# Second block, second layer: mixing by blocks of 128 tokens inside the expert stages, and modulation sums on VectorE

## The chip, the core and the metric

The kernel runs on one core of one Trainium2 chip. The time is that of the device for one execution, in microseconds (us). The engines are TensorE (PE, its weight loads PEld), VectorE (DVE), ScalarE (ACT), GpSimd (POOL) and SyncE (SP, which issues the plain DMAs). All arithmetic that matters is fp32.

## What is computed

A first block (two layers of a transformer over 256 tokens and 256 context tokens, 1024 features) is followed by a second block of two layers. What matters here:

```python
# first block, each layer: shifts, scales and gates from the conditioning vectors
m = silu(cond) @ w_mod + b_mod            # 6 parts of 1024, for c and for c_ctx
h = rms_norm(x, norm_mix) * (1 + sc1) + sh1

# second block, each of 2 layers, x is 256 x 1024
x = x + mixing(rms_norm(x, norm1_g))      # 3 kinds of heads, all causal, then w_out
x = x + peer(rms_norm(x, norm2_g))

# mixing: z = xn @ w_in; 6 stick-breaking attention heads, 6 mLSTM heads in
# chunks of 128 (with a causal conv of width 4 ahead), 4 spatial gating groups in chunks of 128

# peer (the expert layer), for each token and each of 8 heads
q = xn @ wq;  scores against two sets of 128 keys
top 16 of each, top 16 of their 256 sums -> 16 experts idx and gate = softmax
act = xn . u[idx];  w = gelu(act) * gate;  y += sum_k w[k] * v[idx[k]]
```

Every part of the mixing is causal or works within 128 tokens: tokens 0 to 127 never need anything of tokens 128 to 255. The expert layer treats each token by itself.

## The kernel before

**Program.** The first block (to about 1000 us) is written stage by stage. The second block is `block2` (L759): for each layer `mixing` (L765), `norm2_first` (L742) and `peer` (L1076), one after another. The order of the mixing of a layer is a written list (`MIXING`, L1246); it works on all 256 tokens with features on partitions, and each weight tile is split into two halves of fp32r that are multiplied in three passes (`mm3`, L169 to L171; the split on ACT L133 and DVE L134).

**Expert layer** (`peer`). It goes over 2 token blocks times 8 heads times 8 pairs. A pair is two gathers on POOL (L1152), each bringing for 128 tokens one expert's row of u and v (8 KB a token, 1.05 MB a gather) into one of the 8 `b16` buffers, of which two are held for the layer, so that 6 serve the gathers. DVE multiplies u by the tokens, held in the PSUM tile `xt`, and sums (L1156). `weigh` (L1131), one pair behind, makes the gelu'd and gated weight a diagonal matrix on ACT (L129, tile `lo`), and PE adds weight times v onto the two banks `y` (L1140, four matmuls of 512 columns). The lists of experts of a head come from `routed` (L1116) and `route` (L1202, some 30 small DVE instructions); for the first block of tokens `scores` (L1098) also multiplies two weight tiles, loaded through the three `raw` buffers. Two heads are routed before the first pair, each other two heads ahead. `peer_out` (L1171) turns y into the feature layout and adds it to x. Nothing of the next layer's mixing starts before that.

**Modulation** of the first block. Parts 0 and 1 of layer 0 (`mod_first`, L222) are computed inside the first layer's start, with the weights `w_mod0` loaded there. Parts 2 to 5 of layer 0 (`mod_step`, L246) are 32 weight tiles that are fed one by one between other stages, each by two PE matmuls with two stationary columns (L264). Layer 1's parts go through `mod_sum` (L270): DVE multiplies each tile by a column and adds (L126), and only the sums over partitions are matmuls (L288). `mod_out` (L292) transposes the result and adds the bias. `pow_rsqrt` (L314) is the inverse root, a power on POOL (L319).

**Order.** Each engine runs its instructions in the order of its own list; the lists are made when the program is built, by a scheduler that may move an instruction ahead of others in program order.

Of the kernel before, what the change touches and what calls it, by code (L numbers as in the profile page):

```python
# [19 lines left out]
P = 128  # L20
# [46 lines left out]
class Kernel:  # L67
    def __init__(self, tc, ctx, d, out):
        self.tc, self.nc, self.d, self.out = tc, tc.nc, d, out
        self.n = 0  # L70
        self.ahead = []
        self.hold = []
        self.pool = ctx.enter_context(tc.tile_pool(name="sb", bufs=1))
        self.pp = ctx.enter_context(tc.tile_pool(name="ps", bufs=1, space=bass.MemoryType.PSUM))
        self.pp2 = self.scope = None
        self.psum_pool()
# [6 lines left out]
    def psum(self, tag):  # L83
        pool = self.pp2 if tag == "sm" else self.pp
        return pool.tile([P, 512], F32, tag=tag, name=self.name(tag), bufs={"mm": 3, "sm": 4, "ax": 1}[tag])
# [55 lines left out]
    def raw(self, ap):  # L141
        n = ap.shape[-1]
# [71 lines left out]
    def mod_setup(self):  # L214
# [5 lines left out]
        self.mod_ps = None  # L220

    def mod_first(self, q):  # L222

        w = self.b16([P, KD, 512])
        for k in range(0, KD, 4):
            self.nc.sync.dma_start(w[:, k:k + 4], self.d["w_mod0"][q, :, k:k + 4])
        ps = self.psum("ax")
# [6 lines left out]
        pt = self.psum("mm")  # L234
        for j in range(4):
            self.transpose(pt[:, j * P:(j + 1) * P], rows[:, j * P:(j + 1) * P])
        p4 = pt.rearrange("p (c j r) -> p c j r", c=2, r=P)
        blk = slice(2 * q, 2 * q + 2)
        mod = self.mods[0][:, :2, blk]
        self.tt(mod, p4[:, :, :, :2], self.b_mod[:, 0, :2, blk, None].to_broadcast([P, 2, 2, 2]), OP.add)  # L240
        for g in range(32, P, 32):
            self.tt(mod, p4[:, :, :, g:g + 2], mod, OP.add)
        g = self.cols["norm_mix"]
        self.stt(mod[:, 1], mod[:, 1], 1.0, g[:, 0, blk, None].to_broadcast([P, 2, 2]), OP.add, OP.mult)

    def mod_step(self, n=1):  # L246


        for _ in range(n):
# [5 lines left out]
            if l:  # L255
                self.mod_sum(l, c, k)
                continue
            if k == 0:
                self.mod_ps = self.psum("ax")
                self.nc.vector.memset(self.mod_ps, 0.0)  # L260
            w = self.raw(self.d["w_mod"][self.mod_pos - 17])
# [4 lines left out]
            if k < 7:  # L266
                continue
            self.mod_out(l, c, lambda p3, half: [p3[:, :, 32 * half + o:32 * half + o + 2] for o in (0, 64)])

    def mod_sum(self, l, c, k):  # L270

        if k == 0:
            self.mod_acc = self.s8([P, 2, D])
        w = self.raw(self.d["w_mod"][self.mod_pos - 17])
        acc = self.mod_acc
        for i in range(2):
            if k == 0:
                self.ts(acc[:, i], w, self.sc[:, k, i:i + 1], None, OP.mult)
            else:
                self.stt(acc[:, i], w, self.sc[:, k, i:i + 1], acc[:, i], OP.mult, OP.add)  # L280
# [4 lines left out]
        for i in range(2):  # L285
            for half in range(2):
                g = 32 * (2 * half + i)
                self.nc.tensor.matmul(self.mod_ps[g:g + 1, :], self.ones[:, :1],  # L288
                                      acc[:, i, half * 512:half * 512 + 512], start=True, stop=True)
        self.mod_out(l, c, lambda p3, half: [p3[:, :, 64 * half:64 * half + 64:32]])  # L290

    def mod_out(self, l, c, parts):  # L292
# [7 lines left out]
        mod = self.mods[l][:, c]  # L300
        for half in range(2):
            m = mod[:, 4 * half:4 * half + 4]
            add = self.b_mod[:, l, c, 4 * half:4 * half + 4, None].to_broadcast([P, 4, 2])
            for part in parts(p3, half):
                self.tt(m, part, add, OP.add)
                add = m
        if c in (1, 4):
# [1120 lines left out]
```

## Time and profile before

| quantity | value |
|---|---|
| median of 3 runs | 2931.26 us (2930.69 to 2934.92) |
| the profiled execution | 2938.2 us |
| its span, first to last instruction | 2936.4 us |
| PE, DVE, ACT, POOL busy | 87%, 66%, 36%, 19% of the span |
| mean granted clock of PE | 0.968 |
| moved by DMA | 776.35 MB, of it 536.90 MB by the gathers |

The first block ends at about 1000 us, the mixing of layer 0 takes until about 1340 us, the gathers of layer 0 run from 1380.2 us to 2053 us, the mixing of layer 1 lies between, and the gathers of layer 1 run from 2243 us to the end. The busy shares are means over stages with different limits, so a stage is read from the slices and windows below, and the reason for a wait from the groups of instructions, where each line ends with the idle time ahead of it and what released it.

### The profile page before, as it was taken

Reading aid. Unit: us, or ns where it says so; the run is one execution under the profiler, and the core shown is the slowest. Engines: PE = TensorE matmul, PEld = TensorE weight load, DVE = VectorE, ACT = ScalarE, POOL = GpSimd, SP = SyncE. Lnnn points to the kernel's source line nnn. Section 1 sums busy time; section 2 is a strip of 40 time slices with the busy share of each in tenths; the row PEclk is TensorE's granted clock in tenths of the full one; section 3 lists DMA queues with packets and bytes.
Section 4 is the critical chain, followed back from the end, with each engine's and each line's share of the span. In section 5 each row is a group of like instructions: output and inputs, shape, how many; then the busy total and the mean of one; then the engine's idle time right before and its main releaser. Section 6 shows DMA issues by size and latency. Waiting matters only on the chain.

```text
span 2936.4 us, 33987 instructions
## 1 busy us (share of the span) xinstructions
PE 2565.1 (87%) x11870; PEld 1750.2 (60%) x11870; DVE 1937.0 (66%) x4272; ACT 1057.4 (36%) x2173; POOL 551.1 (19%) x559
## 2 busy tenths in 40 slices
PE   6999999999999999997788878777997888687777
PEld 4666777888788999986444323322886444232222
DVE  4434659997375887577667769555577776975554
ACT  3333334442264565464323323111554332421111
POOL 0000000000000000102343333332112333233332
PEclk9999999999999999999999998999998999989999
DMA  6432235555343456433999999999426999889998
GB/s 247 144 134 86 79 110 191 187 189 175 115 138 108 155 185 200 150 108 139 418 418 419 418 420 395 419 420 384 132 72 242 418 418 419 349 360 420 420 420 354
DMA packets 140569, 776.35 MB, mean 264 GB/s; under 512 B 15728, under 2 KB 18800, under 8 KB 73328
## 3 DMA queue, kind: packets, MB, share of 16 engines
q0 software_dynamic: 73728, 536.90, 44.4%
q1 hardware_dynamic: 66672, 237.28, 24.2%
q8 instruction: 95, 1.56, 0.2%
q14 instruction: 74, 0.61, 0.1%
HBM read 773.08 MB, written 1.05 MB: 264 GB/s over the span
## 4 chain that ended last, share of the span: by engine, by line
PE 29%; DMA 23%; DVE 14%; ACT 2%; issue 2%; POOL 1%; POOLq 0%; ACTq 0%; DVEq 0%; SPq 0%
DMA b<-in_peer_uv_dram,b 20%; PE y L1140 8%; PE mm L169 5%; PE mm L170 5%; PE mm L171 5%; DVE b L1156 5%; DMA raw<-in_peer_wq_dram 4%; DVE t L117 2%; PE sm L45 1%; DVE t L1197 1%; DVE b L1200 1%; PE mm L45 1%; DVE b L1199 1%; ACT hi L133 1%; DVE lo L134 1%
## 5 line engine op out<-in xcount | busy, mean ns | idle before, releaser
L1140 PE MATMUL y<-b,lo 128*128 128x512 f32 x2048 | 976.7, 628 | 279.8 <-ACT lo L129 279.8
L1140 PEld LDWEIGHTS y<-b,lo 128*128 128x128 f32 x2048 | 394.8, 200 | 832.6 <-issue 418.9
L1156 DVE SCALAR_TENSOR_TENSOR b<-xt,b 128x1024 f32<-128x1024 f32 x512 | 620.0, 1221 | 273.8 <-DMA b<-in_peer_uv_dram,b 271.6
L1152 POOL DMA_INDIRECT b<-in_peer_uv_dram,b x512 | 500.5, 978 | 854.2 <-DMA b<-in_peer_uv_dram,b 347.5
L134 DVE TENSOR_TENSOR lo<-raw,hi 128x1024 fp32r<-128x1024 f32 (+1 forms) x339 | 406.1, 1199 | 298.9 <-ACT hi L133 269.9
L133 ACT ACTIVATE hi<-raw 128x1024 fp32r<-128x1024 f32 (+1 forms) x339 | 351.8, 1039 | 562.3 <-PE mm L170 278.4
L169 PE MATMUL mm<-b,hi 128*128 128x512 f32 (+1 forms) x1512 | 528.6, 351 | 4.0 <-ACT b L129 1.5
L170 PE MATMUL mm<-b,hi 128*128 128x512 f32 (+1 forms) x1512 | 525.3, 348 | 0.0
L171 PE MATMUL mm<-b,lo 128*128 128x512 f32 (+1 forms) x1512 | 525.1, 348 | 0.0
L319 POOL TENSOR_TENSOR c<-c,k_mhalf 128x4 f32<-128x4 f32 (+2 forms) x39 | 45.1, 1156 | 1502.4 <-DVE c L123 1501.6
L169 PEld LDWEIGHTS mm<-b,hi 128*128 128x128 f32 x1512 | 285.8, 189 | 54.8 <-issue 6.5
L171 PEld LDWEIGHTS mm<-b,lo 128*128 128x128 f32 x1512 | 286.3, 189 | 37.7 <-issue 2.7
L170 PEld LDWEIGHTS mm<-b,hi 128*128 128x128 f32 x1512 | 286.3, 189 | 37.7 <-DVE b L126 2.6
L129 ACT ACTIVATE b<-b 128x2 f32<-128x2 f32 (+2 forms) x280 | 61.8, 221 | 672.5 <-DVE b L1156 664.8
L169 PE MATMUL mm<-s,hi 128*128 128x256 f32 (+2 forms) x976 | 285.4, 295 | 7.3 <-ACT s L133 5.1
L171 PE MATMUL mm<-s,lo 128*128 128x256 f32 (+2 forms) x976 | 282.5, 293 | 0.0
L170 PE MATMUL mm<-s,hi 128*128 128x256 f32 (+2 forms) x976 | 280.4, 289 | 0.9 <-DVE s L134 0.6
L129 ACT ACTIVATE lo<-k_sq,b 128x128 f32<-128x128 f32 x512 | 178.6, 394 | 179.2 <-DVE b L117 173.8
L169 PEld LDWEIGHTS mm<-s,hi 128*128 128x128 f32 (+1 forms) x976 | 188.2, 194 | 17.0 <-ACT s L133 6.8
L170 PEld LDWEIGHTS mm<-s,hi 128*128 128x128 f32 (+1 forms) x976 | 188.3, 193 | 5.6 <-issue 2.4
L171 PEld LDWEIGHTS mm<-s,lo 128*128 128x128 f32 (+1 forms) x976 | 187.8, 194 | 3.6 <-issue 2.6
L117 DVE TENSOR_TENSOR b<-b 128x2 f32<-128x2 f32 (+3 forms) x272 | 45.9, 170 | 102.5 <-ACT b L129 102.4
(241 smaller groups left out, 2361.1 us busy)
## 6 DMA issues: line engine op xcount, KB each, us to landing
raw<-in_w_in_dram SPq DMA_DIRECT2D x97, 512.0 KB, 3.4
raw<-in_w_up_dram SPq DMA_DIRECT2D x88, 512.0 KB, 3.3
raw<-in_w_mod_dram SPq DMA_DIRECT2D x80, 512.0 KB, 3.6
raw<-in_w_out_dram SPq DMA_DIRECT2D x32, 512.0 KB, 3.3
raw<-in_w_down_dram SPq DMA_DIRECT2D x32, 512.0 KB, 3.6
raw<-in_peer_wq_dram SPq DMA_DIRECT2D x32, 512.0 KB, 8.5
b<-in_w_mod_dram SPq DMA_DIRECT2D x8, 1024.0 KB, 12.4
raw<-in_w_br_dram SPq DMA_DIRECT2D x16, 512.0 KB, 3.3
```

The lines of the kernel that those rows point to most:

```text
L45: ins = k.nc.tensor.matmul(out, lhsT, rhs, start=first is None, stop=True, skip_group_check=True)
L117: self.nc.vector.tensor_tensor(out, a, b, op=op)
L129: self.nc.scalar.activation(out, in_, fn, **kw)
L133: return (self.nc.scalar.activation(hi, x, AF.Copy), self.nc.vector.tensor_tensor(lo, x, hi.bitcast(F32), op=OP.subtract))
L134: self.nc.vector.tensor_tensor(lo, x, hi.bitcast(F32), op=OP.subtract))
L169: mm(ps, sh, mh, start=first, stop=False)
L170: mm(ps, sh, ml, start=False, stop=False)
L171: mm(ps, sl, mh, start=False, stop=last)
L319: self.nc.gpsimd.tensor_tensor(r[:, :n], v[:, :n], self.mhalf[:, :n], op=OP.pow)
L1140: nc.tensor.matmul(bank["y"][c], dg[:, i], rows[:, i, D + 512 * c:D + 512 * (c + 1)], start=h == 0 and k + i == 0, stop=h == 7 and k + i = ...
L1152: nc.gpsimd.indirect_dma_start(out=rows[:, i], out_offset=None, in_=table[:, :], in_offset=bass.IndirectOffsetOnAxis(ap=part["idx"][:, tb, ...
L1156: self.nc.vector.scalar_tensor_tensor(rows[:, i, :D], bank["x"], 1.0, rows[:, i, :D], op0=OP.mult, op1=OP.mult, accum_out=part["act"][:, t ...
```

## The change

The expert layers and layer 1's mixing become four `stage`s, (layer, token block): (0,0), (0,1), (1,0), (1,1). A stage is the 64 pairs of one block; behind each pair it takes `rate` steps of a generator of other work. `first_routes` (layer 0's scores and routes) runs beside (0,0), the mixing of tokens 0 to 127 for layer 1 and their routes (`mixed(0)`) beside (0,1), those of tokens 128 to 255 (`mixed(1)`) beside (1,0). `mixed` keeps tokens on partitions, and multiplies with the weight as the moving operand in plain fp32 (`rows_product`), without the split into halves; the weights, the keys and the constants are loaded anew for each block of tokens where `mixed` asks for them. x is held token by token (`xtm`), and the expert result is added and sent from there. The `b16` tile `stream` is held too. The tokens that DVE multiplies come from SBUF (`part["x"]`) instead of PSUM.

In the first block parts 2 to 4 of layer 0's modulation become DVE sums by halves (`mod_half`) and part 5 goes by `mod_sum`; the tiles of `w_mod0` and the first three of `w_vu` are loaded at the program's start.

```diff
     def mod_step(self, n=1):
...
-            if l:
+            if l == 0 and c < 5:
+                self.mod_half(c, *divmod(k, 4))
+            else:
                 self.mod_sum(l, c, k)
-                continue
...
-            for half in range(2):
-                g = 32 * (2 * (k % 2) + half)
-                self.nc.tensor.matmul(self.mod_ps[g:g + 2, :], self.sc[:, k, :], w[:, half * 512:half * 512 + 512],
-                                      start=k < 2, stop=k >= 6)
...
+    def mod_half(self, c, half, pair):
+
+        w = self.raw(self.d["w_mod"][self.mod_pos - 17])
+        for i in range(2):
+            self.mod_add(self.mod_parts, w[:, 512 * i:512 * i + 512], 2 * pair + i)
+        if pair < 3:
+            return
...
     def block2(self, x, xn):
-        for l in range(DEPTH):
-            self.mixing(l, x, self.norm2(x, self.cols["norm1"][:, l], 3) if l else xn)
-            x = self.peer(l, x)
-            self.psum_pool(l + 1 == DEPTH)
...
+        self.mixing(0, x, xn)
+        self.experts(x)
+        self.psum_pool(True)
...
+        first = self.first_routes(x, xf, xn, q, later)
+        self.run(first, (0, 0, 1))
+        self.stage(0, 0, first, 0.5)
+        mix = [self.mixed(b) for b in range(2)]
+        self.stage(0, 1, chain(first, mix[0]), 1.5)
+        self.stage(1, 0, chain(mix[0], mix[1]), 1.6)
+        self.stage(1, 1, mix[1], 1)
...
+    def stage(self, l, tb, work, rate):
...
+        for h in range(8):
+            self.run(work, (l, tb, h))
             for k in range(0, 16, 2):
                 rows = self.b16([P, 2, 2 * D])
...
                 for i in range(2):
-                    self.nc.vector.scalar_tensor_tensor(
-                        rows[:, i, :D], bank["x"], 1.0, rows[:, i, :D], op0=OP.mult, op1=OP.mult,
-                        accum_out=part["act"][:, tb, h, k + i:k + i + 1])
+                    nc.vector.scalar_tensor_tensor(
+                        rows[:, i, :D], part["x"], 1.0, rows[:, i, :D], op0=OP.mult, op1=OP.mult,
+                        accum_out=part["act"][:, h, k + i:k + i + 1])
...
+                behind.append((h, k, rows))
+                due += rate
+                while n + 1 <= due:
+                    next(work, None)
+                    n += 1
...
+    def rows_product(self, xT, units, n, per=2):
...
+        for ap in units:
+            w = self.raw(ap)
+            for i in range(per):
+                self.nc.tensor.matmul(ps, xT[:, k], w[:, i * n:(i + 1) * n], start=k == 0, stop=k == KD - 1)
+                k += 1
+            if k < KD:
+                yield
```

How the lists of the engines change, at three places. On PE, beside the gathers of the second block of tokens of layer 0, before:

```order
L1140 MATMUL y_14315<-b_2571_14419,lo_14438 128x512
L1140 MATMUL y_14316<-b_2571_14419,lo_14438 128x512
L1140 MATMUL y_14315<-b_2571_14419,lo_14438 128x512
L1140 MATMUL y_14316<-b_2571_14419,lo_14438 128x512
L1140 MATMUL y_14315<-b_2573_14433,lo_14452 128x512
L1140 MATMUL y_14316<-b_2573_14433,lo_14452 128x512
```

The same place now (`mm` is the bank of a product, `raw` a weight tile, `s` the turned tokens):

```order
L1156 MATMUL y_14678<-b_2648_14754,lo_14778 128x512
L1156 MATMUL y_14679<-b_2648_14754,lo_14778 128x512
L1156 MATMUL y_14678<-b_2648_14754,lo_14778 128x512
L1156 MATMUL y_14679<-b_2648_14754,lo_14778 128x512
L1247 MATMUL mm_14768<-raw_14791,s_2634_14690 128x512 x2
L1247 MATMUL mm_14768<-raw_14809,s_2634_14690 128x512
L1156 MATMUL y_14678<-b_2652_14773,lo_14800 128x512
L1156 MATMUL y_14679<-b_2652_14773,lo_14800 128x512
L1156 MATMUL y_14678<-b_2652_14773,lo_14800 128x512
L1156 MATMUL y_14679<-b_2652_14773,lo_14800 128x512
```

Between the four matmuls of one pair and those of the next now stand about three of the mixing, each of which needs a weight tile that SP has loaded. On POOL, a little into the second block of tokens, before (a gather's target is a buffer `b`, two gathers each row):

```order
L1152 DMA b_2542_14262<-in_peer_uv_dram,b_2230_12417 128x2048 x2
L1152 DMA b_2552_14317<-in_peer_uv_dram,b_2230_12417 128x2048 x2
L1152 DMA b_2553_14323<-in_peer_uv_dram,b_2230_12417 128x2048 x2
L1152 DMA b_2555_14337<-in_peer_uv_dram,b_2230_12417 128x2048 x2
L1152 DMA b_2567_14391<-in_peer_uv_dram,b_2230_12417 128x2048 x2
```

And now, with the first inverse root of `mixed(0)` (`c` is a column of sums):

```order
L1164 DMA b_2620_14631<-in_peer_uv_dram,b_2240_12506 128x2048 x2
L1164 DMA b_2623_14655<-in_peer_uv_dram,b_2240_12506 128x2048 x2
L1164 DMA b_2630_14674<-in_peer_uv_dram,b_2240_12506 128x2048 x2
L333 TENSOR_TENSOR c_2628_14670<-c_2627_14668,k_mhalf_75 128x1
L1164 DMA b_2641_14712<-in_peer_uv_dram,b_2240_12506 128x2048 x2
L1164 DMA b_2644_14730<-in_peer_uv_dram,b_2240_12506 128x2048 x2
```

Its input `c_2627` is written on DVE directly behind the second multiply of b_2623, so two gathers (b_2630) are issued beyond the data that DVE has by then. There are ten such roots in the stages. On DVE, at the 51st pair of stage (0,0), before:

```order
L117 TENSOR_TENSOR b_2230_12417<-b_2230_12417 128x2
L1156 SCALAR_TENSOR_TENSOR b_2496_14000,b_2230_12417<-xt_12613,b_2496_14000 128x1024 x2
L117 TENSOR_TENSOR b_2230_12417<-b_2230_12417 128x2
L1156 SCALAR_TENSOR_TENSOR b_2508_14054,b_2230_12417<-xt_12613,b_2508_14054 128x1024 x2
L117 TENSOR_TENSOR b_2230_12417<-b_2230_12417 128x2
```

And now:

```order
L1168 SCALAR_TENSOR_TENSOR b_2554_14289,b_2240_12506<-b_2240_12506,b_2554_14289 128x1024
L119 TENSOR_TENSOR b_2240_12506<-b_2240_12506 128x2
L1647 TENSOR_REDUCE sv_14422<-t_2579_14414 128x32
L1604 MAX sv_14454<-b_2218_12390 128x8
L128 SCALAR_TENSOR_TENSOR b_2240_12506<-sv_14422 128x16
L1604 MAX sv_14454<-b_2218_12390 128x8
L1605 MATCH_REPLACE t_2586_14453<-sv_14454,b_2218_12390 128x128
L1607 MAX_INDEX b_2240_12506<-sv_14454,b_2218_12390 128x8
L1606 MAX sv_14454<-t_2586_14453 128x8
L1605 MATCH_REPLACE t_2586_14453<-sv_14454,b_2218_12390 128x128
L1608 MAX_INDEX b_2240_12506<-sv_14454,t_2586_14453 128x8
L1168 SCALAR_TENSOR_TENSOR b_2554_14289,b_2240_12506<-b_2240_12506,b_2554_14289 128x1024
```

All 16 routes of layer 0 now lie in stage (0,0), half a route beside each of 20 pairs in a row (pairs 34 to 53); before, four pairs of layer 0 near there and ten at the second block's start had so much.

## Rows read from the trace of the kernel before

**Rows 1.** Page, the span in 40 slices of 73 us: tenths, GB/s
```profile
PE   6999999999999999997788878777997888687777
DVE  4434659997375887577667769555577776975554
PEclk9999999999999999999999998999998999989999
DMA  6432235555343456433999999999426999889998
GB/s 247 144 134 86 79 110 191 187 189 175 115 138 108 155 185 200 150 108 139 418 418 419 418 420 395 419 420 384 132 72 242 418 418 419 349 360 420 420 420 354
```
**Rows 2.** Windows: busy us (x count) of PE, PEld, DVE, ACT, POOL; PEclk, DMA share, GB/s
```profile
200.00:400.00 200.00, 198.57 (x999) 150.29 (x998) 104.00 (x184) 68.34 (x120) 0.00 (x0) 1.00 0.27 91
1400.00:1500.00 100.00, 82.55 (x299) 46.75 (x298) 62.90 (x174) 30.66 (x78) 36.32 (x35) 0.95 1.02 418
1900.00:2000.00 100.00, 74.38 (x161) 28.75 (x160) 51.80 (x100) 17.93 (x60) 37.09 (x40) 1.00 1.01 420
2100.00:2200.00 100.00, 99.01 (x661) 84.81 (x660) 70.65 (x150) 57.37 (x121) 14.50 (x12) 1.00 0.30 101
2500.00:2600.00 100.00, 67.71 (x129) 27.79 (x130) 98.31 (x388) 40.71 (x86) 28.17 (x31) 0.86 0.84 327
```
**Rows 3.** Groups, 1900 to 2000 us: busy, mean ns, idle ahead and releaser
```profile
L1140 PE MATMUL y<-b,lo 128*128 128x512 f32 x161 | 74.6, 605 | 25.6 <-ACT lo L129 25.6
L1152 POOL DMA_INDIRECT b<-in_peer_uv_dram,b x40 | 37.6, 939 | 63.2 <-DMA b<-in_peer_uv_dram,b 60.0 <-issue 3.1
```
**Rows 4.** Chain between the layers: start, length, step
```profile
2052.96 1.25 DVE b L1156 x2
2250.58 1.25 DVE b L1156 x2
```
**Rows 5.** Windows of L264 alone, sum over 60 to 500 us
```profile
sum 440.00, PE 35.74 PEld 3.15; mean PE 11.91 PEld 1.05
```
**Rows 6.** Groups, 400 to 600 us
```profile
L126 DVE SCALAR_TENSOR_TENSOR s<-raw,k_sc,s 128x1024 f32<-128x1024 f32 x46 | 58.4, 1278 | 0.0
L288 PE MATMUL ax<-s,k_sq 128*1 128x512 f32 x24 | 3.1, 590 | 0.0
```
**Rows 7.** Groups of PE, 1990 to 2240 us
```profile
L138 PE MATMUL sm<-k_sq,t 128*128 128x128 f32 x28 | 5.1, 280 | 0.7 <-DVE t L114 0.7
```
**Rows 8.** Waits of PE, 0 to 80 us: in all, times, longest
```profile
PE sm L169 <- ACT b L129: 5.2, 2, 4.3
PE ax L231 <- DMA b<-in_w_mod_dram: 2.0, 3, 1.4
```
**Rows 9.** DMA, 1400 to 1600 us: queue and share; issues and us to landing
```profile
q1 hardware_dynamic: 2160, 5.90, 7.5%
raw<-in_peer_wq_dram SPq DMA_DIRECT2D x8, 512.0 KB, 8.8
```
**Rows 10.** Groups, 2500 to 2600 us
```profile
L1156 DVE SCALAR_TENSOR_TENSOR b<-xt,b 128x1024 f32<-128x1024 f32 x33 | 39.9, 1213 | 0.0
L1152 POOL DMA_INDIRECT b<-in_peer_uv_dram,b x31 | 29.1, 940 | 72.1 <-PE y L1140 60.5 <-issue 4.9 <-DVE b L1156 4.8
```
**Rows 11.** Two lines over the span: ns min/median/max, first and last start
```profile
L1152 POOL DMA_INDIRECT b<-in_peer_uv_dram,b x512: 935/939/1805, 1380.2 to 2907.0; - x171
L1156 DVE SCALAR_TENSOR_TENSOR b<-xt,b x512: 1203/1224/1227, 1386.2 to 2926.7; 128x1024 f32<-128x1024 f32 x171
```
**Rows 12.** Page, costliest groups: the power on POOL
```profile
L319 POOL TENSOR_TENSOR c<-c,k_mhalf 128x4 f32<-128x4 f32 (+2 forms) x39 | 45.1, 1156 | 1502.4 <-DVE c L123 1501.6
```
**Rows 13.** Two lines, 1500 to 1600 us: ns min/median/max
```profile
L134 DVE TENSOR_TENSOR lo<-raw,hi x4: 1210/1225/1227, 1525.3 to 1571.1; 128x1024 fp32r<-128x1024 f32 x4
L1152 POOL DMA_INDIRECT b<-in_peer_uv_dram,b x36: 935/939/1804, 1501.4 to 1595.9; - x36
```
**Rows 14.** Chain, 1390 to 1460 us: start, length, step
```profile
1398.32 11.34 DMA raw<-in_peer_wq_dram
1426.84 17.45 PE y L1140 x40
```

More of the change, by code (lines that the diff above doesn't have):

```diff
@@ L404, in block1 @@
         self.mod_setup()
+        self.mod_w, raws = [], []
+        for u in range(4):
+            self.mod_w.append(self.mod_load(u))
+            if u < 3:
+                raws.append(self.raw(d["w_vu"][0, u]))
+        self.raws = raws
         self.sink = self.sb([P, DEPTH, 8], "k_sink")
@@ L1093, in peer @@
             c += 8 * n
         for name in ("pos", "si", "idx"):
-            part[name] = part[name].bitcast(U32)
-        now = {}
-        def scores(h):
-            nonlocal q
-            c0 = 0 if h else 1
-            if h:
-                q = self.t2([P, 2, T])
-            for c in range(c0, 2):
-                self.copy(q[:, c], self.fm(self.unit(d["peer_wq"][l, 2 * h + c]), xn, 0, KD, 0, T))
-            keys = self.raw(d["peer_keys"][l, h].rearrange("p c n -> p (c n)")).rearrange("p (c n) -> p c n", c=2)
-            ps = self.psum("mm")
-            for tb in range(2):
-                for c in range(2):
-                    nc.tensor.matmul(ps[:, tb * T + c * P:tb * T + (c + 1) * P], q[:, c, tb * P:(tb + 1) * P],
-                                     keys[:, c], start=True, stop=True)
-            s = now[h] = self.t2([P, 512])
-            self.copy(s[:, :T], ps[:, :T])
-            self.copy(later[:, h], ps[:, T:])
@@ L1116, in routed @@
-        def routed(tb, h):
-            if tb == 0:
-                scores(h)
-                s = now.pop(h)
-                src, tmp = s[:, :T], s[:, T:]
-            else:
-                src, tmp = later[:, h], self.t2([P, 512])[:, :T]
-            self.route(tb, h, src, tmp, part)
-        units = [(tb, h) for tb in range(2) for h in range(8)]
-        routed(*units[0])
-        routed(*units[1])
+            self.part[name] = self.part[name].bitcast(U32)
+        self.done = set()
+        stream = self.b16([P, 4096])
@@ new lines, in experts, with run @@
+        self.xtm = stream[:, :2 * D].rearrange("p (b c) -> p b c", b=2)
+        self.kept = stream[:, 2 * D:]
+        first = self.first_routes(x, xf, xn, q, later)
[5 more added lines that the diff above has]
+        self.stage(1, 1, mix[1], 1)
+    def run(self, work, key):
+        while key not in self.done:
+            next(work)
@@ L1128, in peer, with weigh @@
+    def stage(self, l, tb, work, rate):
+        nc = self.nc
+        table = self.d[f"peer_uv{l}"]
+        part = {n: p[:, tb] for n, p in self.part.items()}
+        y = None
         behind = []
-        bank = {}
-        def weigh(tb, h, k, rows):
-            w = part["w"][:, tb, h, k:k + 2]
-            self.tt(w, w, part["e"][:, tb, h, k:k + 2], OP.mult)
+        due = n = 0.0
+        def weigh(h, k, rows):
+            w = part["w"][:, h, k:k + 2]
+            self.tt(w, w, part["e"][:, h, k:k + 2], OP.mult)
@@ L1159, in peer @@
                     if i == 0 and behind:
+                        if y is None:
+                            y = [self.pp2.tile([P, 512], F32, tag=f"y{c}", name=self.name("y"), bufs=1)
+                                 for c in range(2)]
                         weigh(*behind.pop())
-                self.act(part["w"][:, tb, h, k:k + 2], part["act"][:, tb, h, k:k + 2], AF.Gelu_apprx_tanh)
-                behind.append((tb, h, k, rows))
-                if k == 4 and n + 2 < len(units):
-                    routed(*units[n + 2])
```

537 lines of the change are left out of this document (454 added, 83 removed).

## The prediction

> **What bounds the kernel now.** I read the slices of the page first, then windows of 100 us in each stage, then groups and the chain for the waits. The slices [rows 1] show three regimes: PE full and DMA a quarter to a half used (slices 2 to 18, the first block and the first mixing); DMA full at 418 to 420 GB/s with PE at 7 or 8 tenths (the gathers of both layers); and between them, in slices 29 to 31, PE full again and DMA down to 72 GB/s. The windows say it more sharply [rows 2]: at 1900 us DMA is at 1.01, PE at 74%, DVE at 52%; at 2100 us, in the second layer's mixing, PE is at 99% and DMA at 0.30. So the program alternates between a stage that only PE holds and one that only DMA holds, and the change puts one beside the other. Inside the quiet gathers 40 land in 100 us (POOL waits 60 of 100 us for data), so a pair takes 5.0 us; PE works 74.6 us of the 100 on y, 3.73 us a pair, and waits 25.6 us for the diagonals of ScalarE, 1.28 us a pair [rows 3].
>
> **The change part by part.** The sum is made against the profiled execution, 2938.2 us; the median is 6.9 us less, and this is taken off at the end.
>
> *The gap.* The last multiply of layer 0 starts at 2052.96 and the first of layer 1 at 2250.58, 197.6 us later [rows 4]. In quiet gathers two such are 2.5 us apart (100/40), so what goes is **-195 us**. It goes whole only if the new work ends inside its stages. By the steps it does: each `mixed` yields some 90 times, and a stage of 64 pairs takes 96 or 102 steps, so the first route that stage (1,0) needs is due about pair 46 and the last about pair 60.
>
> *What the mixing brings into the gathers.* Its weights come once for each block of tokens: 46 tiles of 0.524 MB, 4 of 0.432, 4 key tiles of 0.262, together 26.9 MB, and 28.9 MB with the first block's constants. Against that, 14 query tiles and 7 key tiles that stood inside layer 1's gathers go (8.3 MB). Net 47.5 MB. When the plain queue moved 5.90 MB it took 7.5% of 200 us [rows 9], 393 GB/s: **+121 us**. At the 420 GB/s of a quiet window it is 113, at the 327 of the crowded one [rows 2] 145: these are its ends.
>
> *Does PE fit?* y is 3.73 us a pair. The mixing has 88 matmuls of 512 columns a block; at y's price of 0.93 us each (3.73/4) that is 82 us, and with the shorter products, some 50 transposes at 0.28 us [rows 7] and the heads I estimate 125 us, 1.95 us a pair. Together 5.7 us, against DMA's (134.2 + 28) MB / 0.419 = 387 us for 64 pairs, 6.05 us. PE fits, barely. In the window at 1400 us, where query products stood beside gathers, PE was at 83% and DMA still full [rows 2]. But PE takes its list in order, and between two pairs' y now stand matmuls that need a weight tile. What this costs is not shown by any row, so bounds: nothing (the 1400 us window), and 0.9 us for every pair, if the 1.28 us of waiting stays and isn't filled (1.28 + 3.73 + 1.95 - 6.05), 115 us in 128 pairs. I take **+20**, 10 us a stage, near the low end because the window is the nearest row.
>
> *The roots on POOL.* Nine of the ten roots stand in POOL's list with two gathers issued beyond the data that DVE has multiplied (one has eleven, and costs nothing). While POOL waits, no gather is issued. From a gather's issue to its multiply is 6.0 us [rows 11]; with the multiply of 1.22 us ahead, some 0.5 us of small instructions and 1.16 us for the power [rows 12] the next gather lands 8.9 us after the one that DVE was given, where three gathers in sequence take 7.5 us. So 1.4 us for each, more where DVE lags behind the data: **+15** for nine, from 0 (the weights fill the hole) to 50 (DVE 4 us late each time).
>
> *The routes.* A route is some 6.6 us of DVE. In 2500 to 2600 us DVE is at 98%, only 31 gathers are issued instead of 40 [rows 2, 10]: 9 x 2.5 = 22 us lost, which goes, since layer 1's routes are spread over the mixing. In exchange stage (0,0) has half a route beside each of 20 pairs in a row: 2.45 + 3.3 + 0.5 = 6.3 us of DVE against 5.0 of data, 1.3 x 20 = 25 us, less 4 that were lost at the smaller bunch of before: +21. Together **-1** (from -22, if the buffers hide the new one, to +10).
>
> *The multiply.* With one operand in PSUM it takes 1.224 us [rows 11]. Of two SBUF operands the nearest row is the modulation's, 1.278 us [rows 6], 0.054 more. It counts where DVE decides, in some 54 pairs: 108 x 0.054 = **+6**; elsewhere DVE waits for data 42% of the time. [...] All 512 multiplies get two SBUF inputs beside gather issues on POOL; if DVE lost the 0.94 us of an issue at 4 in 10 of those 108, the term would be 41 us more (an estimate). Where the trace has the same pairing, at 1500 us, the subtraction of two SBUF tiles never took over 1.227 us while a gather issue took up to 1.804 [rows 13]: POOL waits, which is idle 60% of the time, and DVE doesn't.
>
> *Front.* In 200 to 400 us PE is busy 198.57 of 200 us [rows 2], so a matmul taken away shortens the program. The 32 units of L264 take 35.74 us [rows 5]; three of them fill a pause of the norm near 415 us and are worth nothing: -32. Back come the partition sums: a whole one has 8 records, and 24 take 3.1 us [rows 6], so one whole and six halves are 4; 12 more transposes at 0.28 us are 3; three multiplies of 1.278 us that now stand on DVE ahead of the modulated x in that pause, 2; and DVE, at 52% there, gets 24 units of 2.7 us, whose sums PE may have to wait for, 4. **-19**, from 0 to -35.
>
> *Start.* The tiles for the first modulation are loaded ahead. PE's waits there are 2.0 us on that DMA and 5.2 on its first normed tokens [rows 8]: **-5**, from 0 to -11.
>
> Sum: -195 + 121 + 20 + 15 - 1 + 6 - 19 - 5 = -58. 2938.2 - 58 = 2880; less 6.9, **2873 us**.
>
> **Rivals.**
> *Everything hides* (the five gather buffers cover the roots, PE's waits and the new bunch). For it: 1400 us, with DMA at 1.02. Against it: one buffer fewer than before, and DMA did fall when DVE was crowded. -58 - 20 - 15 - 21 = -114: 2817 us.
> *Weight tiles land late.* There are three `raw` buffers. A tile landed after 8.8 us beside the gathers [rows 9], the slowest in the chain after 11.34 [rows 14]; with some 4 us until PE has read it, three buffers give one each 4.3 to 5.1 us, where 1.5 steps a pair of 6.05 us ask for one each 4.0. Over 46 tiles 1.1 us is 48 us a stage, PE's y behind it late with it. Against it: ends of products take steps without a tile and let the loads catch up, which gives back about half. 48 in place of 20: 2901 us.
> *Slower: PE's list in order becomes the bound.* Each pair's y waits for its diagonal as now, the mixing's matmuls come behind it and wait again for tiles or for DVE and ACT, and nothing fills the holes. That is the high end above, 115 in place of 20: 2968 us. It decides from 58/128 = 0.45 us a pair beyond my 0.16. For it: 25.6% of idle time on PE in quiet gathers with only y to do. Against it: that idle time is there because DMA is the bound, and when y had fallen behind, 40 of its matmuls' records went through in one go of 17.45 us, 3.5 us a pair [rows 14].
> *The mixing is not done inside its stages*, and part of the gap stays: if a third did, +65, 2938 us. Against it: the count of steps.
>
> **How the numbers follow.** Forecast 0.55, all hidden 0.18, tiles late 0.12, PE's order 0.13, gap stays 0.02. A measurement of this kernel tells about 0.2%, 6 us, from no change. Faster by more (under 2925.4): nearly all of the first two, and most of the third, 0.81; slower: the fourth and part of the last, 0.14; within, 0.05. The forecast's own range is 2840 to 2905. The whole range goes from the all-hidden case, 2808, to 2942, which holds late tiles and part of PE's order.
>
> **What would show it.** No stretch of 200 us with PE at 99% and DMA at 0.3 between the layers; in the mixed stages DMA over 0.95 for most slices and about 390 us for each. If all hides, the whole expert part shows 420 GB/s throughout, stage (0,0) included. If tiles are late, PE's waits there name `raw`; if PE's order rules, POOL's gathers wait for y and the mixed stages take over 440 us each. Dips of DMA behind each root on POOL would be the holes priced at 1.4 us. In 60 to 500 us PE should show no L264 and the stretch be 15 to 25 us shorter. The prediction is wrong if a mixed stage takes over 430 us, or if the first route of a stage comes after its gathers should start.

## The result, and the profile after

The changed kernel takes 2949.97 us, median of 5 runs (2945.64 to 2954.27), the kernel before in the same series 2933.59 (2930.69 to 2936.92): ratio 1.0057, 95% interval 1.0042 to 1.0072. It is slower by 16 us; 2873 was forecast. The profiled execution of the changed kernel took 2949.7 us, its span is 2947.9, and the sum of the prediction stood at 2880 for it: 70 us are missing.

The gap between the layers is gone, as [rows 1] would have to show it. The same slices of the changed kernel:

```profile
PE   7999989999999999996878679788878888877777
DVE  6874789994556786677565974554863454975554
DMA  7541246664434566427898799989989979999998
GB/s 268 172 145 59 86 143 187 186 195 133 134 118 133 165 202 181 126 93 284 338 386 344 295 395 398 383 339 416 418 323 387 391 261 396 418 413 420 420 420 338
```

No slice between the layers falls to 72 GB/s any more. But from slice 19 on, where [rows 1] mostly had 418 to 420 within a layer, only the last stage holds that; the rest wavers between 261 and 418. Windows of 200 us in stages (0,0), (0,1) and (1,0), columns as in [rows 2]:

```profile
1400.00:1600.00 200.00, 154.74 (x507) 83.20 (x508) 118.57 (x325) 54.49 (x140) 63.61 (x58) 0.89 0.87 349
1800.00:2000.00 200.00, 168.66 (x454) 78.83 (x453) 99.76 (x221) 70.70 (x153) 79.72 (x65) 0.95 0.94 376
2200.00:2400.00 200.00, 168.86 (x488) 81.70 (x486) 91.34 (x202) 80.48 (x158) 67.20 (x57) 0.96 0.95 377
```

The first of them is the surprise. It has no mixing beside it, only the same kind of queries and routes that stood there before, and moves 349 GB/s where the kernel before moved 418 [rows 2], with PE less busy too. The stages end to end show how much that is. These four rows of DVE's timeline (start, length) are the first multiplies of the four stages:

```profile
1359.13 1.23 DVE L1168 SCALAR_TENSOR_TENSOR b<-b,b 128x1024 f32<-128x1024 f32 x1 [0.73 <-DMA b<-in_peer_uv_dram,b]
1762.21 1.23 DVE L1168 SCALAR_TENSOR_TENSOR b<-b,b 128x1024 f32<-128x1024 f32 x1 [0.92 <-DMA b<-in_peer_uv_dram,b]
2179.09 1.23 DVE L1168 SCALAR_TENSOR_TENSOR b<-b,b 128x1024 f32<-128x1024 f32 x1
2617.29 1.23 DVE L1168 SCALAR_TENSOR_TENSOR b<-b,b 128x1024 f32<-128x1024 f32 x1 [0.93 <-DMA b<-in_peer_uv_dram,b]
```

All stage times below are differences of such starts (where a layer or the program ends, the last multiply and 2.5 us), each from the one profiled execution of its kernel. Stage (0,0) has the same code in four kernels of the table (after, roots on ScalarE, a quarter of the weights, modulation back on PE) and took 401.5 to 411.8 us in them, so a stage time alone tells a difference from about 10 us on.

| kernel | median us | (0,0) | (0,1) | (1,0) | (1,1) |
|---|---|---|---|---|---|
| before (same blocks of tokens) | 2933.59 | 347.7 | 321.6 | 368.7 | 312.4 |
| after, by the prediction's terms | 2873 | 369 | 817 for both | | 320 |
| after | 2949.97 | 403.1 | 416.9 | 438.2 | 323.2 |
| six buffers in (0,0) | 2942.22 | 406.3 | 417.0 | 437.1 | 323.2 |
| before, one buffer fewer | 2962.59 | 358.8 | 327.1 | 379.6 | 316.9 |
| roots on ScalarE | 2915.00 | 401.5 | 403.4 | 414.4 | 321.7 |
| a quarter of the weights | 2901.69 | 404.4 | 399.1 | 409.6 | 322.1 |
| three steps at a time | 2929.41 | 391.1 | 417.1 | 431.7 | 323.2 |
| spread thinner | 2952.21 | 422.7 | 411.5 | 423.1 | 323.2 |
| spread thinner, roots on ScalarE | 2932.33 | 420.7 | 407.2 | 412.8 | 322.0 |
| modulation back on PE | 2969.67 | 411.8 | 416.2 | 438.2 | 323.2 |
| heads two ahead | 2910.59 | 372.7 | 420.4 | 429.2 | 323.2 |
| heads two ahead, roots on ScalarE | 2879.99 | 366.1 | 412.5 | 412.0 | 323.8 |
| three steps, roots on ScalarE | 2897.62 | 387.9 | 404.7 | 413.7 | 322.0 |
| heads two ahead, roots on ScalarE, mixing four steps at a time | 2895.41 | 363.5 | 420.7 | 423.5 | 323.5 |

The prediction's stages are worked out so: (0,0) is that of before and the 21 us of the new bunch of routes; the two mixed ones are 2 x 320, 55.8 MB at 393 GB/s, 20 for PE and 15 for the roots. So (0,0) is 34 us over, the mixed stages 38, the last 3; the front is 3 better. Within rounding that is the missing 70.

### The profile page after: what moved, and what is told of

Read it like the earlier page. It is cut to its first block, busy times and chain, and to the rows that moved or that the text cites. A ratio compares the mean times of both kernels' runs of the same rounds, so it can differ in the third digit from the quotient of the medians.

```text
span 2947.9 us, 32295 instructions
## 1 busy us (share of the span) xinstructions
PE 2558.4 (87%) x11082; PEld 1682.4 (57%) x11082; DVE 1933.8 (66%) x4277; ACT 1063.1 (36%) x2119; POOL 693.5 (24%) x550
## 4 chain that ended last, share of the span: by engine, by line
PE 30%; DMA 21%; DVE 12%; ACT 4%; issue 3%; POOL 2%; POOLq 0%; ACTq 0%; SPq 0%; DVEq 0%
DMA b<-in_peer_uv_dram,b 16%; PE y L1156 11%; PE mm L173 4%; PE mm L174 4%; PE mm L175 4%; DVE b L1168 4%; DMA raw<-in_peer_wq_dram 2%; PE mm L1247 2%; DMA raw<-in_w_c_dram 2%; PE sm L45 2%; DVE t L119 1%; ACT L131 1%; POOL b L1164 1%; DVE t L1605 1%; DVE b L1607 1%
## 5 line engine op out<-in xcount | busy, mean ns | idle before, releaser
L1168 DVE SCALAR_TENSOR_TENSOR b<-b,b 128x1024 f32<-128x1024 f32 x512 | 621.4, 1222 | 333.6 <-DMA b<-in_peer_uv_dram,b 333.1
L1164 POOL DMA_INDIRECT b<-in_peer_uv_dram,b x512 | 642.7, 1255 | 783.1 <-PE y L1156 410.1
L135 ACT ACTIVATE hi<-raw 128x1024 fp32r<-128x1024 f32 (+1 forms) x289 | 300.0, 1038 | 485.9 <-PE mm L174 283.6
L136 DVE TENSOR_TENSOR lo<-raw,hi 128x1024 fp32r<-128x1024 f32 (+1 forms) x289 | 345.8, 1197 | 192.9 <-ACT hi L135 190.0
L131 ACT ACTIVATE b<-b 128x2 f32<-128x2 f32 (+3 forms) x269 | 57.3, 213 | 666.5 <-DVE b L1168 659.5
L1247 PE MATMUL mm<-raw,s 128*128 128x512 f32 (+2 forms) x416 | 186.2, 577 | 31.6 <-DMA raw<-in_w_q_dram 8.5
L173 PE MATMUL mm<-s,hi 128*128 128x256 f32 (+1 forms) x712 | 205.4, 291 | 4.8 <-ACT s L135 2.6
L175 PE MATMUL mm<-s,lo 128*128 128x256 f32 (+1 forms) x712 | 208.1, 294 | 0.0
L174 PE MATMUL mm<-s,hi 128*128 128x256 f32 (+1 forms) x712 | 204.2, 288 | 0.4 <-DVE s L136 0.3
L128 DVE SCALAR_TENSOR_TENSOR s<-raw,k_sc,s 128x1024 f32<-128x1024 f32 (+1 forms) x182 | 183.3, 1031 | 6.1 <-DMA raw<-in_w_mod_dram 6.0
L1247 PEld LDWEIGHTS mm<-raw,s 128*128 128x128 f32 x416 | 76.3, 190 | 131.0 <-issue 81.6
```

Of the source, the lines that this page charges most:

```text
L128: self.nc.vector.scalar_tensor_tensor(out, a, s, b, op0=op0, op1=op1)
L131: self.nc.scalar.activation(out, in_, fn, **kw)
L135: return (self.nc.scalar.activation(hi, x, AF.Copy), self.nc.vector.tensor_tensor(lo, x, hi.bitcast(F32), op=OP.subtract))
L136: self.nc.vector.tensor_tensor(lo, x, hi.bitcast(F32), op=OP.subtract))
L173: mm(ps, sh, mh, start=first, stop=False)
L174: mm(ps, sh, ml, start=False, stop=False)
```

## The experiments

**The theories.** A: too few gather buffers. B, later split into D and E: the order of the extra work in stage (0,0) (D: query tiles that come one at a time; E: too much work for each pair). C: the roots on POOL, priced too low. The rival of late weight tiles and that of PE's list stayed open too.

**Six buffers in stage (0,0).** The tile `stream` is taken where the first routes end.

```diff
-        stream = self.b16([P, 4096])
...
+        stream = self.stream = self.b16([P, 4096])
+        self.xtm = stream[:, :2 * D].rearrange("p (b c) -> p b c", b=2)
+        self.kept = stream[:, 2 * D:]
+        for b in range(2):
+            tokens(self.xtm[:, b], x, b)
+            yield
```

> The changed kernel, with one edit: the buffer that holds x token by token is taken at the end of the first routes instead of in their middle, so stage (0,0) has six pair buffers for its gathers throughout, as the kernel before had, instead of five from its 14th pair on. The other stages keep five. Theory A (too few gather buffers: with five the waits of the lists in order are no longer covered): stage (0,0), 403 us from its first multiply to the next stage's, falls to about 365, and the whole from 2950 to about 2912 (2900 to 2925). Theory B (the new order itself costs it, half routes beside the pairs and steps between them): 2950 within 6.

2942.22 us (2936.92 to 2954.01), ratio to before 1.0030 (1.0018 to 1.0043); stage (0,0) 406.3 us in its profile, which caught the longest of the six runs, 2954.01. Theory A had asked for about 38 us and falls as the main cause in this stage: the median is 8 us less, and the profile shows no shorter stage. Whether the sixth buffer is worth those 8 us here stays open.

**The kernel before with one buffer fewer.**

```diff
         route = self.b16([P, 2, 2048])
+        spare = self.b16([P, 4096])
+        nc.vector.memset(spare[:, :1], 0.0)
...
+        nc.vector.tensor_copy(spare[:, :1], part["w"][:, 1, 7, 15:16])
         return x
```

> The kernel before, with one b16 buffer held and unused through each expert layer: five pair buffers instead of six while a layer's queries are multiplied, six instead of seven after. Theory A: the 8-pair stretches beside the queries go from 41 to 44 us to about 54, as in the changed kernel's stage (0,0): five such stretches in each layer, 50 us a layer, the second blocks unchanged: 2933 becomes about 3030 (2990 to 3050). Theory B: 2933 within 6.

2962.59 us (2959.80 to 2969.57), 29 more than before, ratio 1.0100 (1.0083 to 1.0117). In the kernel before, a buffer is worth 11 us in a stage with routes (358.8 against 347.7, 379.6 against 368.7) and about 5 in one without: a price that the prediction had left out, and a third of what theory A needed.

**Roots on ScalarE.** In the mixed stages only, at both places where they take a root (the first is shown; `sm_bufs` is 2 from the expert layers on):

```diff
-        self.nc.gpsimd.tensor_tensor(r[:, :n], v[:, :n], self.mhalf[:, :n], op=OP.pow)
+        if self.sm_bufs == 2:
+            self.act(r[:, :n], v[:, :n], AF.Ln)
+            self.act(r[:, :n], r[:, :n], AF.Exp, scale=-0.5)
+        else:
+            self.nc.gpsimd.tensor_tensor(r[:, :n], v[:, :n], self.mhalf[:, :n], op=OP.pow)
```

> The changed kernel with the ten inverse roots of the mixed stages taken off POOL: a logarithm and an exponential on ScalarE instead (some 0.4 us each and up to two table loads of 1.28 us). Theory C (POOL standing before a root empties the gathers in flight; the trace shows 3 to 4 us more than a usual spacing at the next multiply): about 30 us less, 2920 (2910 to 2930), all of it in stages (0,1) and (1,0). Theory A: the buffers empty there anyway, 2950 within 8, or slower by the table loads, up to 2970.

2915.00 us (2909.94 to 2919.39), 35 less than the changed kernel, ratio to before 0.9946 (0.9929 to 0.9963); (0,1) is 13.5 us shorter, (1,0) 23.8, the others as they were. Theory C holds. What the root did is seen in the changed kernel's timeline. POOL's rows (start, length, in brackets what it had waited):

```profile
1747.13 0.95 POOL L1164 DMA_INDIRECT b<-in_peer_uv_dram,b  x1 [3.92 <-PE y L1156]
1748.39 1.55 POOL L1164 DMA_INDIRECT b<-in_peer_uv_dram,b  x1 [0.30 <-issue]
1767.85 1.57 POOL L333 TENSOR_TENSOR c<-c,k_mhalf 128x1 f32<-128x1 f32 x1 [17.91 <-DVE b L119]
1769.61 0.99 POOL L1164 DMA_INDIRECT b<-in_peer_uv_dram,b  x1 [0.19 <-issue]
```

and DVE's multiplies beside them:

```profile
1766.19 1.22 DVE L1168 SCALAR_TENSOR_TENSOR b<-b,b 128x1024 f32<-128x1024 f32 x1
1767.77 1.23 DVE L1168 SCALAR_TENSOR_TENSOR b<-b,b 128x1024 f32<-128x1024 f32 x1
1774.87 1.22 DVE L1168 SCALAR_TENSOR_TENSOR b<-b,b 128x1024 f32<-128x1024 f32 x1
```

POOL stood 17.9 us before the root and issued no gather for 21 us. Its last two gathers had been multiplied, or were being, when the next one was issued, so the next multiply comes 7.1 us after the last and not 2.5. The prediction had counted the two gathers ahead rightly, but from the moment their predecessor landed; DVE was behind the data by then, so they were used up. It had also priced every power at 1.16 us, the mean of [rows 12]. The wider ones take longer:

```profile
1844.68 3.15 POOL L333 TENSOR_TENSOR c<-c,k_mhalf 128x12 f32<-128x12 f32 x1 [18.27 <-DVE c L125]
1974.40 3.77 POOL L1557 TENSOR_TENSOR c<-c,k_mhalf 128x16 f32<-128x16 f32 x1 [12.80 <-DVE c L128]
```

The ten powers of the mixed stages take 22.3 us in all, two of them like the first of these lines and two like the second.

**A quarter of the weights.**

```diff
+        w = self.raw(units[0])
         for ap in units:
-            w = self.raw(ap)
```

> The changed kernel, in which each product of the mixing loads its first weight tile only and multiplies with that tile throughout; 74 tiles of 0.43 to 0.52 MB, 38.5 MB, are left out, all else stays. If the mixed stages are held by the bytes that DMA has to move, they lose 38.5 MB at 393 GB/s, 98 us: 2852 (2845 to 2865), stages (0,1) and (1,0) about 49 us shorter each. If they are held by waits in the order of the lists with too few gathers in flight, the bytes were in the holes: 30 us or less, 2920 or more. The late-tile rival: more than the bytes, 110 us or over, since PE's waits for tiles go too.

2901.69 us (2897.53 to 2902.88), 48 less; (0,1) is 17.8 shorter, (1,0) 28.6. That is between the two expectations and half of the bytes' price: the mixed stages are not held by bytes alone. The other half must have fitted into the holes of the gathers, which this kernel still had, with the roots on POOL. That it isn't over 98 us speaks against late tiles as the main loss.

**Three steps at a time.**

```diff
-                while n + 1 <= due:
-                    next(work, None)
-                    n += 1
+                while n + clump <= due:
+                    for _ in range(clump):
+                        next(work, None)
+                    n += clump
...
-        self.stage(0, 0, first, 0.5)
+        self.stage(0, 0, first, 0.5, 3)
```

> The changed kernel; in stage (0,0) alone the steps of other work are taken three at a time behind every sixth pair instead of one behind every second, so that a head's two query tiles and its route come together, at the same density. Buffers are out after the first runs. Theory D (each query tile, loaded late, makes ScalarE's list stand for its landing ahead of a pair's gelu; together two tiles share one such wait, as in the kernel before): stage (0,0) from 403 to about 375, the whole from 2950 to about 2922. Theory E (it is the density: six heads in 36 pairs and eight routes in 20, where before it was one head for eight pairs): no change, 2950 within 8.

2929.41 us (2923.25 to 2938.86), 21 less, stage (0,0) 12 shorter (stage (1,0), where nothing was changed, came out 6.5 shorter too). D holds in direction, at under half of its size, and the edit did only part of what it was to do. Behind the fourth head `first_routes` takes two steps to turn x into tokens, so from then on the groups of three no longer hold a head's two tiles together. ScalarE's timeline has one pair that lands together and one of the later ones:

```profile
1431.04 1.06 ACT L135 ACTIVATE hi<-raw 128x1024 fp32r<-128x1024 f32 x1 [10.56 <-DMA raw<-in_peer_wq_dram]
1434.83 1.06 ACT L135 ACTIVATE hi<-raw 128x1024 fp32r<-128x1024 f32 x1 [1.38 <-DMA raw<-in_peer_wq_dram]
...
1499.92 1.06 ACT L135 ACTIVATE hi<-raw 128x1024 fp32r<-128x1024 f32 x1 [9.00 <-DMA raw<-in_peer_wq_dram]
1512.37 1.06 ACT L135 ACTIVATE hi<-raw 128x1024 fp32r<-128x1024 f32 x1 [7.95 <-DMA raw<-in_peer_wq_dram]
```

Of the ten query tiles in the stage, ten were waited for over 3 us in the changed kernel, eight in this one, and five in the kernel before.

**Spread thinner.** Three steps for eight pairs (`self.stage(0, 0, first, 0.375, 3)`), the remaining routes among the mixing's steps.

> As the run before, and thinner: in stage (0,0) three steps for every eight pairs, the density of the kernel before, so that only the first three routes of tokens 128 to 255 are made there; the other five stand in stage (0,1), one behind every nine steps of the mixing, at 1.6 steps a pair. The first routes' buffer is held longer, which leaves four gather buffers in the first half of (0,1). Theory E: stage (0,0) about 350 instead of 403, stage (0,1) 10 to 20 longer, whole about 2912. Theory D: as with three steps, and no further gain in (0,0): 375.

2952.21 us (2948.66 to 2956.27), and stage (0,0) 422.7: a miss for both theories, and a bad test of either. The steps that make tokens out of x took places in the queue, and the routes came too late: POOL's waits, 1560 to 1710 us (in all, times, longest), name the instruction that writes the list of experts.

```profile
POOL b L1170 <- DVE b L128: 61.6, 2, 30.8
```

Twice 31 us with no gather issued. The next run is this one with the roots on ScalarE.

> The run before with the ten roots of the mixed stages on ScalarE as in the earlier run, which took 35 us. If the two causes are independent, 35 less than the run before, about 2877; if both are the same idle time of the gathers seen twice, less than 15.

2932.33 us (2929.16 to 2934.03), 20 less, between the two expectations. Perhaps the roots' gain is smaller where the gathers stand for other reasons; no run shows it.

**Modulation back on PE** (parts 2 to 5 of layer 0; the matmuls of L264 and their sums as before).

> The changed kernel with parts 2 to 5 of layer 0's modulation back on PE as before, two matmuls a tile; the tiles of w_mod0 still loaded at the start, the expert part as changed. By the prediction's term the sums on VectorE took 19 us away: 2969 (2962 to 2975), and the first multiply of the experts at about 1378 instead of 1359. Rival: the 27 us that the front gained came mostly from the earlier loads: 2958 or less.

2969.67 us (2957.35 to 2972.42), 20 more; one of the four runs, 2957, would fit the rival. The first multiply starts at 1373.8 us in its profile, against 1359.1 of the changed kernel and 1386.2 before [rows 11]. Stage (0,0), where nothing was changed, came out 8.7 us longer in this profile, so not all of the 20 is the front.

**Heads two ahead.** In stage (0,0) a whole head behind the third pair of each head, as `peer` had done; six routes then stand among the steps of `mixed(0)`, one behind every nine (`beside`).

```diff
-        self.stage(0, 0, first, 0.5)
+        self.stage(0, 0, first, 0)
...
-        self.stage(0, 1, chain(first, mix[0]), 1.5)
...
+        self.stage(0, 1, beside(mix[0], first, 9), 1.6)
...
+                if rate == 0 and k == 4:
+                    self.run(work, (0, (h + 2) // 8, (h + 2) % 8))
```

First with the roots on ScalarE:

> The changed kernel with the roots on ScalarE (2915 us) and, in stage (0,0), the first routes taken exactly as the kernel before took them: a whole head, its two query tiles and its route, behind the third pair of each head, two heads ahead; six routes of tokens 128 to 255 stand in stage (0,1), one behind every nine steps of the mixing at 1.6 steps a pair. Unlike the thinner run no gather should wait for its list of experts. If the loss in stage (0,0) is the order of its extra work (spread singly, and denser): (0,0) 350 to 360 instead of 401, (0,1) 10 to 20 longer than 403, whole 2875 to 2890. If it lies in what all variants of the change share there (tokens in SBUF, five buffers): (0,0) stays near 390, whole 2905 or more.

2879.99 us (2878.67 to 2882.01), ratio to before 0.9817 (0.9801 to 0.9834): faster than both kernels, by 54 and 70 us. Stage (0,0) takes 366.1 us, 35 less than with the roots alone and 6 over what was expected; six routes fewer stand in it, for which (0,1) pays 9 us against the run with the roots alone. The slices of its page, DMA's share and GB/s:

```profile
DMA  7551246665443566434999999999999979999998
GB/s 274 170 154 53 88 131 189 187 186 153 132 127 120 159 183 198 145 106 147 418 374 415 394 370 402 403 352 401 413 379 417 412 299 417 418 366 420 420 420 352
```

Then with the roots on POOL:

> The changed kernel with the first routes taken two heads ahead as in the best run so far (2880 us), but the ten roots on POOL again. If order and roots are two causes: 2880 + 35 = 2915 (2905 to 2922), stage (0,0) 366, (0,1) and (1,0) longer by the roots, 425 and 436. If the roots cost only where the order is bad as well: 2895 or less.

2910.59 us (2904.77 to 2914.56), 39 less than the changed kernel. Order and roots nearly add up: 39 and 35 alone, 70 together.

**Three steps, roots on ScalarE.**

> The changed kernel with the roots on ScalarE and three steps at a time in stage (0,0): each alone took 35 and 21 us. Independent: 2894 (2888 to 2900), stage (0,0) 390, (0,1) 403, (1,0) 414.

2897.62 us (2896.34 to 2899.30), as expected.

**The mixing four steps at a time**, on the best version.

> The best run so far (2880 us, first routes two heads ahead, roots on ScalarE) with the steps of the mixing taken four at a time, at the same rate, so that a product's four weight tiles stand together. If single steps beside each pair cost the mixed stages too, as the query tiles did in stage (0,0): each of (0,1) and (1,0), 412 us, falls by 10 or more, 2855. If the mixed stages have only their bytes (385 to 394 us) and the weights are prefetched well enough: no change within 6, or slower, since 16 matmuls of the mixing, 14 us, then stand at once in PE's list ahead of a pair's y: 2890 to 2900.

2895.41 us (2888.67 to 2905.53), 15 more than the best: (0,1) 420.7, (1,0) 423.5. What helps the query tiles hurts here; the 16 matmuls that then stand at once ahead of a pair's y would explain it, but that isn't shown.

## What the order in stage (0,0) did

The waits of 200 us name it (engine, line, releaser: us in all, times, longest). The changed kernel, 1400 to 1600 us:

```profile
PE y L1156 <- ACT lo L131: 45.3, 14, 6.8
DVE b L119 <- ACT b L131: 63.0, 23, 7.8
ACT hi L135 <- DMA raw<-in_peer_wq_dram: 58.0, 8, 9.3
POOL b L1164 <- PE y L1156: 108.2, 21, 12.3
```

The kernel before at the same place after its first gather, 1426 to 1626 us:

```profile
PE y L1140 <- ACT lo L129: 18.3, 9, 2.9
DVE b L117 <- ACT b L129: 26.3, 30, 5.8
ACT hi L133 <- DMA raw<-in_peer_wq_dram: 43.9, 8, 10.5
POOL b L1152 <- PE y L1140: 32.1, 22, 5.7
```

And the best version, 1400 to 1600 us:

```profile
PE y L1166 <- ACT lo L131: 19.0, 9, 3.0
DVE b L119 <- ACT b L131: 30.4, 29, 5.8
ACT hi L135 <- DMA raw<-in_peer_wq_dram: 40.6, 8, 9.5
POOL b L1174 <- PE y L1166: 30.4, 20, 6.9
```

Read each group from the third line up. ScalarE's list has the split of a query tile (`hi`) ahead of a pair's gelu, and stands there until the tile lands. DVE waits for the gelu, PE for the diagonal, POOL for the buffer that PE frees. Each window has eight splits. ScalarE waits longer for them after (58.0 us against 43.9 and 40.6); above all, each of the eight waits stands at a pair of its own, where in the other two kernels four long ones serve two tiles each. ScalarE's timeline before, where a head's two tiles come together:

```profile
1535.64 1.06 ACT L133 ACTIVATE hi<-raw 128x1024 fp32r<-128x1024 f32 x1 [9.45 <-DMA raw<-in_peer_wq_dram]
1536.60 0.19 ACT L129 ACTIVATE b<-b 128x2 f32<-128x2 f32 x1
...
1539.42 1.06 ACT L133 ACTIVATE hi<-raw 128x1024 fp32r<-128x1024 f32 x1 [1.38 <-DMA raw<-in_peer_wq_dram]
```

One wait of 9.45 us serves both. After:

```profile
1486.72 1.06 ACT L135 ACTIVATE hi<-raw 128x1024 fp32r<-128x1024 f32 x1 [8.60 <-DMA raw<-in_peer_wq_dram]
1487.68 0.19 ACT L131 ACTIVATE b<-b 128x2 f32<-128x2 f32 x1
...
1513.33 1.06 ACT L135 ACTIVATE hi<-raw 128x1024 fp32r<-128x1024 f32 x1 [4.79 <-DMA raw<-in_peer_wq_dram]
1514.29 0.19 ACT L131 ACTIVATE b<-b 128x2 f32<-128x2 f32 x1
...
1527.75 1.06 ACT L135 ACTIVATE hi<-raw 128x1024 fp32r<-128x1024 f32 x1 [6.98 <-DMA raw<-in_peer_wq_dram]
1528.71 0.19 ACT L131 ACTIVATE b<-b 128x2 f32<-128x2 f32 x1
```

Three waits in 41 us, a gelu behind each. Why the tile is late stands in the chain of the changed kernel (start, length, step):

```profile
1464.26 1.22 DVE lo L136
1465.54 7.76 DMA raw<-in_peer_wq_dram
1474.58 2.39 DVE b L1168 x4
1477.34 1.24 DVE lo L136
1478.63 8.07 DMA raw<-in_peer_wq_dram
1488.61 5.37 PE y L1156 x8
```

The next tile is asked for when DVE has taken the low part of an earlier one out of its `raw` buffer, and that subtraction stands in DVE's list behind multiplies; then come 8 us of landing. Load, split, gelu, diagonal, y, buffer, gather, multiply, load: a ring through all five engines, in which each list keeps its order.

One more thing stands in the rows of the whole stage, before and after (columns as in [rows 2]):

```profile
1386.00:1734.00 348.00, 281.86 (x860) 141.96 (x860) 236.94 (x660) 99.10 (x260) 134.41 (x134) 0.95 1.01 419
1359.00:1762.00 403.00, 297.91 (x861) 148.27 (x862) 276.35 (x871) 117.76 (x288) 146.90 (x128) 0.89 0.90 359
```

PE waited 108 us for diagonals in this stage, 56 before; its granted clock was 0.89 in the mean, 0.95 before, and as many matmuls kept it busy for 16 us more. A record of a y matmul took 662 ns in the mean of the changed kernel's 200 us above, 613 in those of the kernel before. So part of the longer ring may be slower matmuls; no run separates them from the waits.

## Why the prediction was wrong

- *The gap*: right. The last multiply of (0,1) starts at 2177.5 us and the first of (1,0) at 2179.1; all of the mixing ended inside its stages.
- *The front and the start*: right in sum, by two errors that nearly cancel. The first multiply comes 27.1 us earlier, where 24 were forecast. With the modulation on PE it comes 12.4 earlier, so VectorE's sums gave 14.7 (19 forecast; the medians' 20 holds the longer stage (0,0) as well), and the earlier loads and the rest 12.4 (5 forecast).
- *The routes* is the first step that failed: "Together -1", with +21 for stage (0,0), counted DVE's work beside each pair and nothing else. It left out that the query tiles too were handed out in single steps and at 1.33 heads for eight pairs, and what waits behind their split on ScalarE. The stage lost 55 us against before and not 21. Of that, taking three steps at once gives back 12, and the old order two heads ahead 30 (35 with the roots gone), six of the new bunch's routes among it, which (0,1) then carries. That order also thins the work to one head for eight pairs, and the run that was to tell D from E told neither, so how much of the 30 is tiles that stand together and how much is density isn't separated. Nor is the rest of 18 to 25 us: the 11 us that a buffer was worth in the kernel before may be in it, though a sixth buffer alone gave the changed kernel 8 us at most, and so may the tokens that DVE now reads from SBUF, which no run put back.
- *The roots on POOL* is the second: right in place and mechanism, wrong in size. 15 us were forecast (1.4 for each of nine), 35 measured (3.9 each). DVE was behind the data, as in "DVE 4 us late each time", the high end of 50, and the power took 2.34 us in the mean of the nine and not 1.16. By these two means the longer powers are 11 of the missing 20 us, an estimate.
- *Does PE fit* was perhaps too low. With the roots gone the mixed stages take 817.8 us, where the forecast without roots has 802: 36 beyond gathers and bytes instead of 20. Which wait the 16 belong to isn't shown. In the changed kernel's mixed stages PE's matmuls wait 15 us each for weight tiles, so late tiles don't explain the 70 us (the 48 us a stage of that rival should read 51 by its own 1.1 us for 46 tiles, which changes nothing). PE's list was no general bound either, though POOL's gathers wait for y as that rival had said: by stages 34 of the 70 lie in (0,0), which has no mixing, and 37 us of the mixed stages went with the roots. In time the rival with a left gap (2938) and the slower one (2968) lay nearest; the first is refuted by the gap, the second named the wrong place. The prediction's own sign of being wrong, a mixed stage of over 430 us, came true: (1,0) took 438.2.
- *The bytes*: 121 us, MB over a rate, is not confirmed as a term. The test that left out 38.5 MB got 48 of 98 us back, in stages whose gathers had holes.
- *The multiply*: +6 forecast, nothing measured. The two lines of [rows 11] are now:

```profile
L1164 POOL DMA_INDIRECT b<-in_peer_uv_dram,b x512: 932/980/2369, 1353.3 to 2918.3; - x171
L1168 DVE SCALAR_TENSOR_TENSOR b<-b,b x512: 1187/1224/1287, 1359.1 to 2938.0; 128x1024 f32<-128x1024 f32 x171
```

The median is the 1224 ns of before, with both operands in SBUF as with one in PSUM; the 1278 of the modulation's row doesn't show. The multiply never takes over 1.287 us, while a gather's issue on POOL takes up to 2.369 us (busy 642.7 us in all, 500.5 before; in the mean of the last stage 1.53 us, 0.94 before). In the last stage, from 2617 us on, the 116 issues that began during a multiply took 1.08 to 1.81 us, the five that didn't 0.94; in the same stage before, with one operand in PSUM, all took 0.94 or 0.95. So POOL gives way, as weighed in the prediction, and none of the 41 us shows on DVE. In the quiet last stage, at 420 GB/s as before, no cost of that shows: what that stage takes longer than before lies in its first eight pairs (41.1 us against 31.3), and from there on eight pairs take 40 to 41 us in both.

So the errors are 34 for stage (0,0), 20 for the roots, 16 in the mixed stages that nothing names, and 0 on balance for the rest. The best version, with the two failed steps taken out, runs in 2880 us, within 7 us of what had been forecast for the change. That nearness is partly luck: the forecast held 15 us for roots and 21 for the bunch in (0,0), which this version doesn't pay, and this version pays 18 in (0,0), 16 in the mixed stages and 9 for the routes in (0,1) that the forecast had not.

## What to carry to other kernels

Work that is put beside a transfer-bound loop needs more than free time on each engine: look in each engine's list for what stands directly ahead of the loop's own instructions, and at what that waits for. On the engine that issues the loop's transfers nothing should stand that waits for data of the loop's present turn: ten tiny powers cost 35 us. And in stage (0,0) loads that arrived one by one ahead of a dependent step each cost their landing (waits of 8.60, 4.79 and 6.98 us), where two asked for together cost one (9.45 us, then 1.38); in the mixed stages, taking four steps together cost 15 us, so this has to be tried at each place.

## What was not expected of the hardware

An inverse root took 1156 ns on POOL in the mean before [rows 12], and in the mixed stages 0.57 to 1.57 us for a single column, 3.15 for 12 and 3.78 for 16. All are small beside the 17.9 us for which POOL stood before one. Taking a buffer of 16 KB a partition from a stage that was already at 418 GB/s cost 3% of it (11 us of 348).
